# The output norm of a tuned encoder block: gains loaded once and multiplied on GpSimd, the last scaling split over VectorE and ScalarE

## Chip, cores, metric

One core of one Trainium2 chip runs the whole kernel. The metric is device time in microseconds, the median of several runs. Engines are called TensorE (PE in the profile), VectorE (DVE), ScalarE (ACT), GpSimd (POOL) and SyncE (SP, which only issues transfers here).

## What is computed

One encoder layer on x of 1 x 2048 x 1024 in float32: an RMS norm, one wide projection, two branches (chunked attention over a band, and retention with a per-head norm), each gated and multiplied by its own output matrix, a gated merge, an output projection with the residual, and a last RMS norm. The change touches the last two lines of this:

```python
def rms_norm(x, gain):
    xf = x.astype(jnp.float32)
    y = xf * lax.rsqrt(jnp.mean(xf * xf, axis=-1, keepdims=True) + NORM_EPS)
    return (y * gain.astype(jnp.float32)).astype(x.dtype)

        branch_a = jnp.einsum('bsf,fd->bsd', o_a * jax.nn.silu(g_a), w_out_attn[l])
        branch_r = jnp.einsum('bsf,fd->bsd', o_r * jax.nn.silu(g_r), w_out_ret[l])
        mixed = jax.nn.sigmoid(m_a) * branch_a + jax.nn.sigmoid(m_r) * branch_r
        x = x + jnp.einsum('bsd,de->bse', mixed, w_out[l]).astype(x.dtype)
    return rms_norm(x, final_gain)
```

## The kernel before

Every matmul keeps float32 accuracy by splitting its operands in a high and a low part (a cast on ScalarE, then a subtraction on VectorE), and the large products are tiled 512 wide. The phases run one behind the other: projections, attention and retention for the first half of the sequence's work, the same for the second, then the merge, opened by `open_phase("mrg", E_MRG, 4)`. The merge runs five jobs in this order: ba0 (attention branch, first half), br0 (retention branch, first half), ba1, br1, and the output projection `out`. Each job goes through chunks of weights. A chunk loads a raw weight tile (`raw`, in a ring of 3), casts it to `wh` (L295, ScalarE) and subtracts to get `wl` (L296, VectorE); its products are 128 x 512, 24 matmuls each in `out`. The names in the traces: raw_ba and wh_ba, wl_ba belong to ba0 and ba1, raw_br and wh_br, wl_br to br0 and br1; ps_ba, ps_br, ps_out are the products in PSUM.

The right operands r lie on chip and are refilled while the phase runs: `refill` (L777 to 782) loads a piece from `yrs` into the low part, casts it (L781) and subtracts (L782). The retention's result passes through `finish_yr` (loads yr, yv, rb, a multiply on VectorE, one on GpSimd at L1067, a store to yrs). The epilogue of a branch product (L1088 for ba) multiplies PSUM with a gate tile ga, which is stored to `tas`; the one of br (L1106, L1107) multiplies with gr and adds ta on GpSimd, and is stored to `mxs`.

The epilogue of an output product is `ep_out` (L1138 to 1158). `before_out` has loaded the rows of x (xr) and the gain (fg, one 1 x 512 piece broadcast to 128 rows), both from ring E. VectorE adds the product to xr (L1143), ScalarE squares and sums into a column of fs (L1149). When the second half of a row block is there, VectorE makes mean and epsilon (L1153, L1154), runs `rsqrt` (L193 to 203, nine small operations: L195, L199, L196, then L202 and L203 three times) and multiplies each half by the result and by the gain (L1158). `put` stores it six steps later, or at the end of the program.

What sets the order: the program is written out step by step while it is recorded. `later(n, fn)` puts a piece of work n steps behind the present one, `put(lag, ...)` a store, and `flush` at the end of a phase emits what is left. Nearly all transfers of this part are issued by SP, in the order in which they were recorded (`dma`); an issue that has to wait holds all behind it. Ring E has E_MRG buffers of 128 x 512 float32 in the merge, and the tiles ga, gr, ta, yr, yv, rb, xr, fg, jk go through it. Before the merge the phase `heads(1)` ends with a chain of operations on rt on VectorE (per-head norm of the retention) and the store of its result to `rss`, which `finish_yr` later loads as rb.

Of the kernel before, what the change touches and what calls it, by code (L numbers as in the profile page):

```python
# [11 lines left out]
F32 = mybir.dt.float32  # L12
# [4 lines left out]
ALU = mybir.AluOpType  # L17
AX = mybir.AxisListType
# [3 lines left out]
P = 128  # L22
SEQ = 2048
DM = 1024
# [9 lines left out]
NORM_EPS = 1e-6  # L34
# [17 lines left out]
E_PROJ = 23  # L52
E_ATT = 16
E_RET = 22
E_MRG = 23
PR_BUFS = 4
ATT_FILLS = (1.0, 1.0)
PV_LAG = 3
# [11 lines left out]
def hybrid_kernel(  # L70
# [24 lines left out]
    small = ctx.enter_context(tc.tile_pool(name="small", bufs=4))  # L95
# [3 lines left out]
    epool, xpool = [None], [None]  # L99
# [10 lines left out]
    def E(name, dt=F32, shape=(P, 512)):  # L110
        return epool[0].tile(list(shape), dt, tag="e", name=name)
# [7 lines left out]
    def open_phase(name, e_bufs, tr_bufs=0):  # L119
        st = ExitStack()  # L120
        phase[0] = st
        epool[0] = st.enter_context(tc.tile_pool(name=f"e_{name}", bufs=e_bufs, reuse_waits="tile"))
        if tr_bufs:
            xpool[0] = st.enter_context(
                tc.tile_pool(name=f"tr_{name}", bufs=tr_bufs, space=PSUM, reuse_waits="tile")
            )
        return st
# [21 lines left out]
    pe, act, dve, pool = Ordered(nc.tensor), Sometimes(nc.scalar), Sometimes(nc.vector), Sometimes(nc.gpsimd)  # L149
    dma = Ordered(nc.sync).dma_start  # L150
# [42 lines left out]
    def rsqrt(v, y, tmp, hv):  # L193

        dve.tensor_scalar(tmp.bitcast(I32), v.bitcast(I32), 1, None, ALU.logical_shift_right)  # L195
        dve.tensor_scalar(  # L196
            y.bitcast(I32), tmp.bitcast(I32), -1.0, RSQRT_MAGIC, ALU.mult, ALU.add
        )
        dve.tensor_scalar(hv, v, -0.5, None, ALU.mult)  # L199
        if v.shape[-1] == 1:  # L200
            for _ in range(3):
                dve.scalar_tensor_tensor(tmp, y, hv, y, ALU.mult, ALU.mult)  # L202
                dve.scalar_tensor_tensor(y, tmp, 1.5, y, ALU.add, ALU.mult)  # L203
            return
        for _ in range(3):
            dve.tensor_tensor(tmp, y, hv, ALU.mult)
            dve.tensor_tensor(tmp, tmp, y, ALU.mult)
            dve.scalar_tensor_tensor(y, tmp, 1.5, y, ALU.add, ALU.mult)
# [32 lines left out]
    def later(n, fn):  # L241

        order[0] += 1
        deferred.append((steps[0] + n, order[0], fn, free[0]))
        deferred.sort(key=lambda e: e[:2])
# [8 lines left out]
    def put(lag, dst, src):  # L254

        later(lag, lambda: dma(dst, src))
# [799 lines left out]
    def finish_yr(h, b, lead):  # L1056

        a, u, r = (E(f"{n}_{h}_{b}") for n in ("yr", "yv", "rb"))
        dma(a, orscr[h // 2][b][h % 2])
        dma(u, urscr[h][b])  # L1060
        dma(r, rsscr[b // 2][8 * b + h].rearrange("(o d) -> o d", o=1).broadcast_to([P, B]))

        def gated():
            dve.scalar_tensor_tensor(a, a, gn[:, h:h + 1], u, ALU.mult, ALU.mult)

        def rest():
            pool.tensor_tensor(a, a, r, ALU.mult)  # L1067
            put(6, yrscr[h][b], a)

        later(lead, gated)  # L1070
        later(lead + 2, rest)
# [52 lines left out]
        b, u = c // 2, c % 2  # L1124
        return mxscr[b][4 * j:4 * j + 4, :, T * u:T * u + T].rearrange("k p t -> p k t")

    rows_out = {}

    def before_out(c, i, j):
        t = 2 * c + j  # L1130
        xr, fg = E(f"xr_{t}_{i}"), E(f"fg_{t}_{i}")
        dma(xr, x[0, t * P:(t + 1) * P, 512 * i:512 * i + 512])
        dma(
            fg, final_gain[512 * i:512 * i + 512].rearrange("(o d) -> o d", o=1).broadcast_to([P, 512]),
        )
        return xr, fg

    def ep_out(c, i, j, src, got):  # L1138

        t = 2 * c + j  # L1140
        xr, fg = got

        dve.scalar_tensor_tensor(xr, src, 0.25, xr, ALU.mult, ALU.add)  # L1143
        if t not in rows_out:
            rows_out[t] = ({}, small.tile([P, 2], F32, tag="fs", bufs=4, name=f"fs_{t}"))
        halves_, fs = rows_out[t]
        halves_[i] = xr, fg
        junk = E(f"jk_{t}_{i}", BF16)
        act.activation(junk, xr, AF.Square, accum_out=fs[:, i:i + 1])  # L1149
        if len(halves_) < 2:  # L1150
            return
        ft, fr, tm, hv = (small.tile([P, 1], F32, tag=f"f{n}", bufs=2, name=f"f{n}_{t}") for n in range(4))
        dve.tensor_reduce(ft, fs, AX.X, ALU.add)  # L1153
        dve.tensor_scalar(ft, ft, 1.0 / DM, NORM_EPS, ALU.mult, ALU.add)  # L1154
        rsqrt(ft, fr, tm, hv)
        for f in range(2):
            o, fg = halves_[f]
            dve.scalar_tensor_tensor(o, o, fr, fg, ALU.mult, ALU.mult)  # L1158
            put(6, out[0, t * P:(t + 1) * P, 512 * f:512 * f + 512], o)


    def attention(s, sbp, ps_wide):
# [442 lines left out]
    for s in range(2):  # L1605
        jobs.append(Job(f"ba{s}", 4, w_stream(w_out_attn, [T * c for c in range(4)], 1), ep_ba(s),
                        kh=1, resident=RYA, before=before_ba(s)))
        jobs.append(Job(f"br{s}", 4, w_stream(w_out_ret, [T * c for c in range(4)]), ep_br(s),
                        resident=RYR, before=before_br(s)))
    jobs.append(Job("out", 8, mx_stream, ep_out, resident=RWO, before=before_out))  # L1610
    end, at = {}, 0
    for j in jobs:
# [82 lines left out]
    strict[0] = False  # L1695

    st = open_phase("mrg", E_MRG, 4)
    for n, (b, h) in enumerate((b, h) for b in range(2, 4) for h in range(HEADS)):
        later(YR_FROM + YR_EVERY * n, lambda h=h, b=b: finish_yr(h, b, 8))
    while step():  # L1700
# [63 lines left out]
```

## Time and profile before

| | |
|---|---|
| time of the runs | 1994.56, 1995.48, 1995.9 us; median 1995.48 us |
| the profiled execution | 1991.62 us, its span from first to last instruction 1989.8 us |
| mean granted clock of TensorE | 0.994 |
| busy share of the span | TensorE 97%, VectorE 69%, ScalarE 45%, GpSimd 44% |
| merge | about 1560 to 1990 us, its out stage 1807.6 to 1981.7 us |

The profile gives, for one execution, what each engine did and when, what ended an idle time (a "releaser"), and a chain followed back from the last instruction. Times in rows are microseconds from the start of the span. A row with x2 or x3 groups neighbouring instructions of the same kind.

### The profile page before, as it was taken

To read this page: it belongs to the slowest core of one execution; us is meant where nothing else is said; L and a number is where in the kernel's file an instruction comes from. 1 tells how busy PE (TensorE), PEld (TensorE's weight loads), DVE (VectorE), ACT (ScalarE), POOL (GpSimd) and SP (SyncE) were. 2 spreads that over 40 slices of the span, in tenths; PEclk is the share of its full clock that TensorE was granted. 3 is DMA by queue.
4 is the path that set the end of the run, shared out by engine and by line. 5 is a ranking of instruction groups with operands and counts; after the bars stand their busy time and mean duration, and the time that the engine had idled before them with its cause. 6 is when DMAs were issued, how large, how long until landed. Compare 5 with 4: busy or idle time off the path is not lost.

```text
span 1989.8 us, 30314 instructions
## 1 busy us (share of the span) xinstructions
PE 1926.7 (97%) x9712; PEld 1604.4 (81%) x9712; DVE 1365.6 (69%) x2603; ACT 899.6 (45%) x1827; POOL 878.7 (44%) x713
## 2 busy tenths in 40 slices
PE   6899999999999999999999999999999999999998
PEld 4687778888888886778788888888888887888886
DVE  7888777777765668888877677765667654534554
ACT  6444554556654555343333555554455311322221
POOL 2544554554556675455654444454675144021000
PEclk9899999999999999999999999999999999999999
DMA  4476796755549987777775645544899999976564
GB/s 148 136 255 210 225 301 205 207 156 165 173 115 282 296 262 259 232 254 237 250 254 173 192 144 168 169 146 137 268 289 281 332 383 372 342 241 216 194 191 138
DMA packets 340910, 447.44 MB, mean 225 GB/s; under 512 B 30776, under 2 KB 194256, under 8 KB 340752
## 3 DMA queue, kind: packets, MB, share of 16 engines
q1 hardware_dynamic: 282688, 388.87, 61.2%
q10 hardware_dynamic: 58064, 56.63, 9.5%
q8 instruction: 78, 1.28, 0.3%
q14 instruction: 80, 0.66, 0.1%
HBM read 294.50 MB, written 150.89 MB: 224 GB/s over the span
## 4 chain that ended last, share of the span: by engine, by line
PE 75%; DVE 9%; DMA 8%; issue 3%; ACT 2%; POOL 2%; SPq 0%; DVEq 0%; ACTq 0%; POOLq 0%
PE ps_g_z L139 7%; PE ps_g_x L139 6%; PE ps_p_z L139 5%; PE ps_p_x L139 5%; PE po L139 4%; PE ps_g_w L139 4%; PE wide L139 4%; PE ps_g_v L139 3%; PE ps_g_y L139 3%; PE o L139 3%; PE tp L139 2%; PE ps_p_w L139 2%; PE ps_p_y L139 2%; PE ps_p_v L139 2%; PE sr L139 1%
## 5 line engine op out<-in xcount | busy, mean ns | idle before, releaser
L139 POOL TENSOR_SCALAR pr<-pr,rsum 128x640 f32<-128x640 f32 (+4 forms) x128 | 97.5, 762 | 233.9 <-DVE rsum L139 99.9
L139 PE MATMUL ps_p_z<-r,wh_p 128*128 128x512 f32 x448 | 145.1, 404 | 6.8 <-DVE u_p L139 5.5
L139 DVE CUSTOM_DVE_ANT_0 pr<-wide,bt 128x640 f32<-128x640 f32 (+4 forms) x128 | 94.3, 736 | 73.7 <-PE wide L139 63.3
L139 PE MATMUL ps_g_z<-r,wh_g 128*128 128x512 f32 x448 | 142.4, 399 | 1.9 <-DVE c_g L139 1.5
L139 PE MATMUL ps_g_x<-r,wh_g 128*128 128x512 f32 x448 | 142.6, 399 | 0.0
L139 PE MATMUL ps_p_x<-r,wh_p 128*128 128x512 f32 x448 | 141.4, 396 | 1.1 <-DVE r L139 1.0
L139 ACT ACTIVATE pr<-pr,mn 128x640 f32<-128x640 f32 (+4 forms) x128 | 98.0, 766 | 80.1 <-DVE mn L139 80.1
L139 POOL TENSOR_TENSOR t_p<-raw_p,t_p 128x512 f32<-128x512 f32 x52 | 78.0, 1501 | 123.7 <-DVE wl_p L139 111.7
L139 DVE TENSOR_TENSOR ptl<-tp,pth 128x384 fp32r<-128x384 f32 x168 | 95.8, 571 | 37.1 <-ACT pth L139 35.5
L139 ACT CAST pth<-tp 128x384 fp32r<-128x384 f32 x168 | 85.5, 515 | 76.2 <-PE tp L139 69.0
L139 POOL TENSOR_TENSOR sl<-sm,sh 128x512 fp32r<-128x512 f32 x64 | 89.2, 1394 | 44.5 <-ACT sh L139 30.9
L1107 POOL TENSOR_TENSOR gr<-gr,ta 128x512 f32<-128x512 f32 x32 | 45.5, 1422 | 140.2 <-DVE gr L1106 135.1
L139 PEld LDWEIGHTS ps_p_z<-r,wh_p 128*128 128x128 f32 x448 | 83.7, 193 | 24.9 <-issue 6.3
L139 DVE TENSOR_TENSOR wl_p<-t_p,wh_p 128x512 fp32r<-128x512 f32 x112 | 101.9, 910 | 1.6 <-ACT wh_p L139 1.6
L139 PEld LDWEIGHTS ps_p_x<-r,wh_p 128*128 128x128 f32 x448 | 83.5, 189 | 19.7 <-DVE r L139 2.6
L139 PEld LDWEIGHTS tp<-ident,pr 128*128 128x128 f32 x560 | 69.6, 140 | 36.8 <-DVE ptl L139 9.0
L139 PE MATMUL tp<-ident,pr 128*128 128x128 f32 x560 | 90.0, 274 | 7.8 <-DVE g L139 2.9
L139 PE MATMUL wide<-ka,qa 128*128 128x512 f32 (+2 forms) x448 | 94.0, 326 | 0.7 <-DVE mn L139 0.7
L139 PE MATMUL po<-pth,va 128*128 128x256 f32 x336 | 92.7, 297 | 0.0
L139 PE MATMUL ps_p_z<-r,wl_p 128*128 128x512 f32 x224 | 89.2, 398 | 0.3 <-DVE wl_p L139 0.3
L139 POOL TENSOR_TENSOR wl_g<-t_g,wh_g 128x512 fp32r<-128x512 f32 x56 | 75.7, 1351 | 31.2 <-ACT wh_g L139 31.1
L139 PE MATMUL ps_p_x<-r,wl_p 128*128 128x512 f32 x224 | 87.9, 393 | 1.0 <-DVE wl_p L139 1.0
(1183 smaller groups left out, 5835.7 us busy)
## 6 DMA issues: line engine op xcount, KB each, us to landing
raw_g<-in_w_in_dram ACTq DMA_DIRECT2D x56, 512.0 KB, 5.4
raw_p<-in_w_in_dram ACTq DMA_DIRECT2D x52, 512.0 KB, 6.2
qa<-qas SPq DMA_DIRECT2D x128, 128.0 KB, 2.9
qr<-qrs SPq DMA_DIRECT2D x128, 128.0 KB, 4.4
vr<-vrs SPq DMA_DIRECT2D x64, 256.0 KB, 5.5
ka<-kas SPq DMA_DIRECT2D x40, 256.0 KB, 3.5
va<-vas SPq DMA_DIRECT2D x40, 256.0 KB, 3.2
kds<-kdt_k SPq DMA_DIRECT2D x32, 256.0 KB, 4.2
```

The source lines that it names most:

```text
L139: return tc.keep_in_program_order(op(*a, **k))
L1107: pool.tensor_tensor(g, g, ta, ALU.add)
```

## The change

The gain is loaded once, at the start of the merge, as two tiles of 128 x 512 with a buffer each, and multiplied by the square root of the width on ScalarE. The 32 loads of fg in `before_out` are gone, and E_MRG is 21 instead of 23, which pays for the two tiles. In `ep_out` GpSimd multiplies each half of xr by its gain into a tile og of ring E, beside the squares. One operation with two columns replaces the sum and the mean (the mean's divisor is in the scaled gain). Half 0 is multiplied by the rsqrt on VectorE, half 1 on ScalarE. The very last store is issued by ScalarE, all others by SP as before.

```diff
-E_MRG = 23
+E_MRG = 21
...
+    def load_gains():
+        for i in range(2):
+            fg = epool[0].tile([P, 512], F32, tag=f"fg{i}", bufs=1, name=f"fg_{i}")
+            gains.append(fg)
+            dma(
+                fg, final_gain[512 * i:512 * i + 512].rearrange("(o d) -> o d", o=1).broadcast_to([P, 512]),
+            )
+            later(14, lambda fg=fg: act.mul(fg, fg, DM ** 0.5))
...
     def before_out(c, i, j):
-        xr, fg = E(f"xr_{t}_{i}"), E(f"fg_{t}_{i}")
+        xr = E(f"xr_{t}_{i}")
         dma(xr, x[0, t * P:(t + 1) * P, 512 * i:512 * i + 512])
-        dma(
-            fg, final_gain[512 * i:512 * i + 512].rearrange("(o d) -> o d", o=1).broadcast_to([P, 512]),
-        )
...
         act.activation(junk, xr, AF.Square, accum_out=fs[:, i:i + 1])
+        og = E(f"og_{t}_{i}")
+        pool.tensor_tensor(og, xr, gains[i], ALU.mult)
+        halves_.append(og)
...
-        dve.tensor_reduce(ft, fs, AX.X, ALU.add)
-        dve.tensor_scalar(ft, ft, 1.0 / DM, NORM_EPS, ALU.mult, ALU.add)
+        dve.scalar_tensor_tensor(ft, fs[:, 0:1], DM * NORM_EPS, fs[:, 1:2], ALU.add, ALU.add)
         rsqrt(ft, fr, tm, hv)
+        dve.tensor_scalar(halves_[0], halves_[0], fr, None, ALU.mult)
+        act.mul(halves_[1], halves_[1], fr)
         for f in range(2):
-            o, fg = halves_[f]
-            dve.scalar_tensor_tensor(o, o, fr, fg, ALU.mult, ALU.mult)
-            put(6, out[0, t * P:(t + 1) * P, 512 * f:512 * f + 512], o)
+            dst = out[0, t * P:(t + 1) * P, 512 * f:512 * f + 512]
+            if t == SEQ // P - 1 and f:
+                act.dma_start(dst, halves_[f])
+            else:
+                put(6, dst, halves_[f])
...
     st = open_phase("mrg", E_MRG, 4)
+    load_gains()
```

The order on the engines moves with it. SP at the start of the merge, before; here r31 and r21 are refilled from yrs, rss is the retention's row chain, and raw_ba0_3 the last weight tile of ba0:

```order
L139 DMA r31_88<-yrs_0_1_327 128x512
L139 DMA ga_4_0_18058<-mas_4_0_374 128x512
L139 DMA r31_88<-yrs_1_1_331 128x512
L139 DMA raw_ba0_3_0_18093<-in_w_out_attn_dram 128x4x256
L139 DMA ga_4_1_18095<-mas_4_1_375 128x512
L139 DMA r31_88<-yrs_3_1_339 128x512
L139 DMA ga_5_0_18115<-mas_5_0_378 128x512
L139 DMA rss_1_464<-rt0_17990 32x512
L139 DMA tas_3_0_434<-ga_3_0_18006 128x512
L139 DMA tas_3_1_435<-ga_3_1_18029 128x512
L139 DMA tas_4_0_438<-ga_4_0_18058 128x512
```

and the same place on SP now:

```order
L139 DMA r31_88<-yrs_0_1_327 128x512
L139 DMA ga_4_0_18058<-mas_4_0_374 128x512
L139 DMA r31_88<-yrs_1_1_331 128x512
L139 DMA rss_1_464<-rt0_17990 32x512
L139 DMA tas_3_0_434<-ga_3_0_18006 128x512
L139 DMA tas_3_1_435<-ga_3_1_18029 128x512
L139 DMA fg_0_18091<-in_final_gain_dram 128x512
L139 DMA fg_1_18093<-in_final_gain_dram 128x512
L139 DMA r31_88<-yrs_2_1_335 128x512
L139 DMA raw_ba0_3_0_18097<-in_w_out_attn_dram 128x4x256
L139 DMA ga_4_1_18099<-mas_4_1_375 128x512
L139 DMA r31_88<-yrs_3_1_339 128x512
```

The store of rss, two of tas and the two gain loads now stand ahead of raw_ba0_3, ga_4_1, yrs_3_1 and (not in these rows) ga_5_0; the load from yrs_2_1, which stood some 35 places earlier before, is behind them too.

VectorE at the same place, now; wl_ba0_3 is made from raw_ba0_3, and the lines L1088 are epilogues of ba0:

```order
L139 TENSOR_TENSOR wl_ba0_2_(1, 0)_18056<-raw_ba0_2_0_17969,wh_ba0_2_(1, 0)_18055 128x512
L1088 SCALAR_TENSOR_TENSOR ga_4_0_18058<-ga_4_0_18058,ps_ba0_2_(0, 0)_18101 128x512
L782 TENSOR_TENSOR r31_88<-r31_88,r30_87 128x512 x2
L296 TENSOR_TENSOR wl_ba0_3_(0, 0)_18117<-raw_ba0_3_0_18097,wh_ba0_3_(0, 0)_18116 128x512
L1088 SCALAR_TENSOR_TENSOR ga_4_1_18099<-ga_4_1_18099,ps_ba0_2_(0, 1)_18121 128x512
L296 TENSOR_TENSOR wl_ba0_3_(1, 0)_18164<-raw_ba0_3_0_18097,wh_ba0_3_(1, 0)_18163 128x512
```

Two subtractions of L782 have come in front of wl_ba0_3; the epilogue of ga_4_1 stands right behind that subtraction, as it did.

VectorE at the very end, now, from the last two epilogues on:

```order
L1150 SCALAR_TENSOR_TENSOR xr_15_0_21396<-ps_out_7_(1, 0)_21447,xr_15_0_21396 128x512
L1150 SCALAR_TENSOR_TENSOR xr_15_1_21445<-ps_out_7_(1, 1)_21480,xr_15_1_21445 128x512
L1162 SCALAR_TENSOR_TENSOR f0_15_21510<-fs_15_21475 128x1
L195 TENSOR_SCALAR f2_15_21512<-f0_15_21510 128x1
L199 TENSOR_SCALAR f3_15_21513<-f0_15_21510 128x1
L196 TENSOR_SCALAR f1_15_21511<-f2_15_21512 128x1
L202 SCALAR_TENSOR_TENSOR f2_15_21512<-f1_15_21511,f3_15_21513 128x1
```

The row L1162 has taken the place of L1153 and L1154. At the end of ScalarE's order stand now the scaling of half 1 and the last store:

```order
L1155 ACTIVATE jk_15_0_21476,fs_15_21475<-xr_15_0_21396 128x512
L1155 ACTIVATE jk_15_1_21506,fs_15_21475<-xr_15_1_21445 128x512
L1165 ACTIVATE og_15_1_21508<-og_15_1_21508,f1_15_21511 128x512
L1169 DMA out_0_dram<-og_15_1_21508 128x512
L1773 UNCONDITIONAL_BRANCH
```

Before, the squares (jk_15_1) were the last work of ScalarE.

## Rows read from the trace of the kernel before

**Rows 1.** The page: busy time by engine.
```profile
PE 1926.7 (97%) x9712; PEld 1604.4 (81%) x9712; DVE 1365.6 (69%) x2603; ACT 899.6 (45%) x1827; POOL 878.7 (44%) x713
```
**Rows 2.** Waits of TensorE, 1560 to 1990: for what, total us, times, longest.
```profile
PE ps_br_(0, 0)_18876 L139 <- ACT wh_br_(0, 0)_18799 L295: 1.5, 1, 1.5
```
**Rows 3.** Busy us by stretch: PE, PEld, DVE, ACT, POOL, clock, DMA share, GB/s.
```profile
1570.00:1585.00 15.00, 15.00 (x67) 12.41 (x67) 9.28 (x16) 4.14 (x7) 1.30 (x1) 1.00 0.87 293
1590.00:1655.00 65.00, 63.54 (x279) 51.97 (x278) 31.42 (x41) 10.16 (x17) 27.86 (x21) 1.00 1.05 384
1807.60:1981.70 174.10, 174.07 (x768) 143.79 (x767) 89.66 (x258) 40.06 (x91) 1.67 (x1) 1.00 0.57 183
```
**Rows 4.** The chain that ended last, from 1981 on: start, us, what.
```profile
1981.71 0.70 DVE xr L1143
...
1983.19 0.17 DVE f L1153
...
1985.29 0.75 DVE xr L1158
1986.04 0.66 DVEq L1760
```
**Rows 5.** The last stores on SP: start, us, what.
```profile
1986.06 0.99 SPq L139 DMA_DIRECT2D out_dram<-xr  x2
```
**Rows 6.** Groups by shape: count, busy us, mean ns, idle before.
```profile
L139 DVE TENSOR_SCALAR xb<-xb,n_b 128x512 f32<-128x512 f32 x4 | 1.7, 482 | 0.0
L139 ACT ACTIVATE xb<-xb,n_b 128x512 f32<-128x512 f32 x4 | 2.6, 712 | 2.3 <-DVE n_b L139 2.3
L202 DVE SCALAR_TENSOR_TENSOR f<-f,f 128x1 f32<-128x1 f32 x48 | 10.5, 220 | 1.7
```
**Rows 7.** GpSimd and VectorE around 1616: start, us, what.
```profile
1616.17 1.29 POOL L1107 TENSOR_TENSOR gr<-gr,ta 128x512 f32<-128x512 f32 x1 [2.43 <-DVE gr L1106]
1616.67 1.33 DVE L1064 SCALAR_TENSOR_TENSOR yr<-yr,gn,yv 128x512 f32<-128x512 f32 x1 [0.58 <-DMA yv<-urs]
```
**Rows 8.** TensorE at 1576, 1587 and 1654: start, us, what.
```profile
1576.63 0.62 PE L139 MATMUL ps_ba_(0, 0)_18195<-r,wh_ba_(0, 0)_18112 128*128 128x512 f32 x2
1587.51 0.62 PE L139 MATMUL ps_br_(0, 0)_18300<-r,wh_br_(0, 0)_18211 128*128 128x512 f32 x2
1654.68 0.73 PE L139 MATMUL ps_br_(0, 0)_18876<-r,wh_br_(0, 0)_18799 128*128 128x512 f32 x2 [1.46 <-ACT wh_br_(0, 0)_18799 L295]
```
**Rows 9.** SP's issues at the start of the merge: start, us, what.
```profile
1563.12 0.44 SPq L139 DMA_DIRECT2D raw_ba<-in_w_out_attn_dram  x1
...
1569.72 0.32 SPq L139 DMA_DIRECT2D rss<-rt  x1
1570.08 1.75 SPq L139 DMA_DIRECT2D tas<-ga  x3
...
1572.42 0.41 SPq L139 DMA_DIRECT2D r<-yrs  x1
1573.58 0.32 SPq L139 DMA_DIRECT2D tas<-ga  x1
1573.99 0.38 SPq L139 DMA_DIRECT2D r<-yrs  x1
...
1578.50 1.53 SPq L139 DMA_DIRECT2D raw_br<-in_w_out_ret_dram  x2
```
**Rows 10.** VectorE: the first subtraction of raw_ba0_3 and the epilogue of ga_4_1.
```profile
1572.26 0.69 DVE L296 TENSOR_TENSOR wl_ba_(0, 0)_18113<-raw_ba,wh_ba_(0, 0)_18112 128x512 fp32r<-128x512 f32 x1 [0.77 <-ACT wh_ba_(0, 0)_18112 L295]
1572.87 0.68 DVE L1088 SCALAR_TENSOR_TENSOR ga<-ga,ps_ba_(0, 1)_18117 128x512 f32<-128x512 f32 x1
```
**Rows 11.** ScalarE's casts that waited for a load: start, us, what.
```profile
1575.43 0.62 ACT L781 CAST r<-r 128x512 fp32r<-128x512 f32 x1 [2.69 <-DMA r<-yrs]
1578.46 0.62 ACT L781 CAST r<-r 128x512 fp32r<-128x512 f32 x1 [2.41 <-DMA r<-yrs]
...
1585.85 0.62 ACT L295 CAST wh_br_(0, 0)_18211<-raw_br 128x512 fp32r<-128x512 f32 x1 [0.96 <-DMA raw_br<-in_w_out_ret_dram]
```

More of the change, by code (lines that the diff above doesn't have):

```diff
@@ L1125, in mx_stream @@
         return mxscr[b][4 * j:4 * j + 4, :, T * u:T * u + T].rearrange("k p t -> p k t")
-    rows_out = {}
+    rows_out, gains = {}, []
+    def load_gains():
[6 more added lines that the diff above has]
+            later(14, lambda fg=fg: act.mul(fg, fg, DM ** 0.5))
     def before_out(c, i, j):
         t = 2 * c + j
-        xr, fg = E(f"xr_{t}_{i}"), E(f"fg_{t}_{i}")
+        xr = E(f"xr_{t}_{i}")
         dma(xr, x[0, t * P:(t + 1) * P, 512 * i:512 * i + 512])
-        dma(
-            fg, final_gain[512 * i:512 * i + 512].rearrange("(o d) -> o d", o=1).broadcast_to([P, 512]),
-        )
-        return xr, fg
+        return xr
     def ep_out(c, i, j, src, got):
         t = 2 * c + j
-        xr, fg = got
+        xr = got
         dve.scalar_tensor_tensor(xr, src, 0.25, xr, ALU.mult, ALU.add)
         if t not in rows_out:
-            rows_out[t] = ({}, small.tile([P, 2], F32, tag="fs", bufs=4, name=f"fs_{t}"))
+            rows_out[t] = ([], small.tile([P, 2], F32, tag="fs", bufs=4, name=f"fs_{t}"))
         halves_, fs = rows_out[t]
-        halves_[i] = xr, fg
         junk = E(f"jk_{t}_{i}", BF16)
         act.activation(junk, xr, AF.Square, accum_out=fs[:, i:i + 1])
+        og = E(f"og_{t}_{i}")
+        pool.tensor_tensor(og, xr, gains[i], ALU.mult)
+        halves_.append(og)
         if len(halves_) < 2:
```

## The prediction, made before the changed kernel ran

> **What bounds the kernel now.** I read the page first. TensorE is busy 97% of the span, the next engine 69% [rows 1]; the granted clock is 1.00, the 2.4 GHz level, in every stretch of [rows 3]. So only two things can move the time: a gap in TensorE's stream, or the work behind its last matmul. I then asked for everything that TensorE waited for from 1560 us to the end, which covers the rest of the retention and the whole merge: one wait, 1.5 us, for a cast of a weight tile [rows 2]. The out stage, where the changed norm sits, runs without a gap: 174.07 us busy in 174.10 [rows 3]. VectorE, ScalarE and GpSimd are busy 52%, 23% and 1% there. What the change takes from VectorE in that stage, and the 32 gain loads that it drops, therefore buys nothing, except behind the last matmul.
>
> Two places are left. **The tail**: the last matmul ends at 1981.7 and the span at 1989.8, so 8.1 us lie bare [rows 4]. **The start of the merge**: from 1590 to 1655 the DMA engines are full (share 1.05, 384 GB/s), and the one wait of TensorE, at 1654.68, is for a weight load that came out of that full queue [rows 2, 3, 8]. A transfer that starts later before 1590 comes out later at 1654. From 1570 to 1585 the share is 0.87, so there is some idle there [rows 3].
>
> **The tail, step by step** [rows 4 to 6]. Before: the epilogue from 1981.71 for 0.70, the squares on ScalarE, the first small operation at 1983.19, ten more of them, scaling of half 0 from 1985.29 for 0.75, its store, scaling of half 1, and the last store (1986.06 and, 0.66 behind the end of half 0, about 1986.7; the two issues fill 0.99). From the last issue to the end are 3.1 us.
> - Of the two operations that make the mean (each 0.17, and gaps of 0.02; they end at 1983.54) one goes; the other becomes a two-input one, which takes 0.17 to 0.22 [rows 4, 6]. Alone that gains 0.14 to 0.19.
> - But GpSimd now multiplies the last half beside the squares. It starts some 0.06 behind the epilogue, at 1982.47, takes 1.29 as in [rows 7], and ends at 1983.76, while the first small operation would start at 1983.19. A row of the merge shows what happens to a VectorE operation of the scalings' kind (0.75 alone [rows 4]) that starts inside such a multiply [rows 7]: begun at 1616.67, it took 1.33 and ended 0.54 after the multiply's end at 1617.46. It did most of its work once GpSimd was through. The small operation reads two columns of SBUF, so I let it wait too. With its whole length behind the multiply it ends at 1983.95, with the 0.2 that the row saved (0.75 - 0.54) at 1983.76; I take 1983.9, where the pair of before ended at 1983.54. The chain is 0.35 *late* instead of 0.17 early; the nine operations behind it run as before, and the rsqrt ends at about 1985.6. The Trainium skill ("SBUF — State Buffer", on the two sides of SBUF) has the rule behind this: a VectorE instruction with two SBUF inputs and a GpSimd instruction that reads SBUF share a port pair, which the one that starts first keeps for its whole length. The row agrees at 512 columns; none shows it for one column, and if that is exempt the tail is 0.5 better than I put it.
> - Half 0: 0.48 on VectorE, by the tensor-by-column rows on 128x512 [rows 6], in place of 0.75, and its store at about 1986.1.
> - Half 1 beside it on ScalarE: 0.71 by the same scaling of 128x512 in the first phase [rows 6]. Done at about 1986.35, and the store is issued by ScalarE's queue, free then, at 1986.37 in place of 1986.7.
> - The other 31 multiplies lie in a stage in which GpSimd is idle. ScalarE's 16 added multiplies (16 x 0.7 = 11 us) lie in 134 us of idle time, and each holds the casts queued behind it for the two to three microseconds of a rsqrt chain, with 5.44 us of TensorE work (174.1/32) for each product in front.
> - What a store from ScalarE's queue costs at the end isn't in the trace: at best as from SP's, at worst some 0.5 more (two issues of SP fill 0.99). I take nothing more, since the bytes are the same.
>
> The tail gains 0.35; ends: 0.2 lost, and 1.2 gained with no hold and a quicker landing of two stores side by side.
>
> **The start of the merge, step by step.** Keeping the gains on chip costs two loads at the phase's start, and these and E_MRG at 21 move other loads. Before, SP issues the load of the last weight tile of the first branch (raw_ba0_3) at 1563.12, with three more loads (ga_4_1, yrs_3_1, ga_5_0), then stands still until 1569.72, when the retention's last row chain has ended on VectorE and rss can be stored [rows 9]. By the order of the built program that store and two of tas, then the two gain loads, now stand *ahead* of these loads, and the load of yrs_2_1 as well, which had been issued long before. Nothing else fills SP's idle time, so five loads (4 x 256 KB and 512 KB) go out later, four of them by some 9.5 us.
> - SP's issues after the stop follow each other at about 0.5 us [rows 9]: rss 1569.72, tas 1570.1 and 1570.6, gains 1571.1 and 1571.6, yrs_2_1 1572.1, raw_ba0_3 1572.6 in place of 1563.1.
> - When does it land? The loads of yrs issued at 1572.42 and 1573.99 had their casts released at 1575.43 and 1578.46 [rows 9, 11], 3.0 and 4.5 us after; raw_ba0_3 is twice as large, so 4.0 to 5.5, I take 4.6: 1577.2. From landing to the first matmul takes 0.7 (a cast of 0.62 [rows 11] and two hand-overs), so 1577.9 against 1576.63 before: TensorE stands 1.3 us there (0.5 to 2.2).
> - On VectorE the subtraction for that tile now stands ahead of ga_4_1's epilogue as before, but waits for it; with the cast at 1577.2, the subtraction follows after 0.65 and the epilogue ends some 1.45 after that starts (1572.26 and 1572.87 with 0.68 before [rows 10]), so at about 1579.3 in place of 1573.55. SP's store of ga_4_1 (tas_4_1) waits for it, and behind that on SP wait the next yrs, ga_6_0, the three loads of the next row, and then the first weight tile of the second branch (raw_br0_0). Before, that store went at 1573.58 and raw_br0_0 at 1578.50 [rows 9], 4.9 later; so it goes at about 1584.2, 5.7 later.
> - What it does to the stream: after 1569.7 the engines have to move 1.5 MB of the five loads and 0.5 MB of gains more ahead of raw_br0_0: 2.1 MB at 384 GB/s, 5.4 us. The idle share from 1570 to 1585, (1.05 - 0.87) x 15 / 1.05 = 2.6 us [rows 3], can take some of it, if SP feeds it. All of it used: the stream is 2.8 late; none used: 5.4. SP is blocked for about 3 us, with some six loads in flight to live on, so I lean to the lower end: 3.2.
> - Before, raw_br0_0 was cast at 1585.85 and wanted at 1587.51 [rows 8, 11], with its weights ready some 0.7 after the cast starts, at 1586.5; 3.2 later that is 1589.7, and TensorE, by then 1.3 late itself, wants it at 1588.8: 0.9 of a wait, 2.2 in all. From there to 1655 the full queue decides: the tile awaited at 1654.68 comes 3.2 later, whatever TensorE lost on the way; the stall there becomes 1.5 + 3.2 - 2.2 = 2.5, or part of it falls on the tiles between. Behind it TensorE waited for nothing [rows 2], so 3.2 reaches the end.
>
> **The sum.** 3.2 - 0.35 = 2.85 us more. The profiled execution takes 1991.62 (span 1989.8), so 1994.5; the median of the runs shown, 1995.48, lies 3.9 above it, and so 1998.3 for the time. A change of under 0.2% (4 us: 1991.5 to 1999.5) can't be told from none here.
>
> **Rivals.**
> A, slower: SP's stop drains the queue. If loads behind the stop take what raw_br0_0 took (issued 1578.50, cast 1585.85: 7.3 us), raw_ba0_3 lands at 1579.9, ga_4_1's epilogue ends at 1582, raw_br0_0 goes at 1586.9 and its cast comes at 1592 (queue filling) to 1594 (queue full), 6 to 8 late; two buffers fewer in the ring push the same way. With 6.4 the sum is +6.05: 2001.5. It decides from a stream 4.3 late on. For it: each step on this path waits for the one ahead, and the queue is full right after. Against it: the 7.3 us are those of a full queue, and behind the stop the rows show 3.0 to 4.5.
> B, absorbed: raw_ba0_3 lands by 1575.9, as the 3.0 us row would give with the idle engines, nobody waits for it, the epilogue of ga_4_1 and so SP's store come at most a few microseconds late, and the stream recovers before 1654. Only the tail counts: 1995.1. For it: 2.6 us of idle share. Against it: 2.1 MB don't fit into that.
> C, the tail is not held: the small operation runs beside the multiply, the rsqrt ends at 1985.1, ScalarE's half at 1985.85, and the tail gains 0.85: 1997.8. For it: the row is not of one column. Against it: the row of two inputs.
>
> **How the numbers follow.** Forecast (the stream 2.5 to 4.3 late, the tail held): 0.42. A 0.30, B 0.17, C 0.11. Time 1998.3. Range: B's 1995.1 less C's 0.5 gives 1994.6; above, A up to a stream 6.8 late, 2001.9. Faster by over 0.2% needs 4 us, and all that could be gained is the tail's 1.2 and the stall's 1.5: 0.04. Slower by over 0.2%: A and the forecast's upper edge, 0.32. Within: 0.64.
>
> **What would show it.** At the start: SP's gap before rss stays, the gain loads stand behind it, raw_ba0_3 is issued near 1572.6, a wait of TensorE of 0.5 to 2 us near 1577 for its cast, another near 1588, and the wait near 1656 for the second branch's last tile moves from 1.5 to about 2.5. The out stage still 174.1 us without a gap. In the tail: a first small operation of 0.7 in place of 0.15 that ends 0.2 behind the multiply, ten small operations in place of eleven, two scalings that overlap, a last issue on ScalarE 4.7 us behind the last matmul in place of 5.0. Wrong: no new wait before 1600 (B), waits of TensorE there that add up to over 4.3 us more than before (A), a first small operation of 0.2 (C), or a gap in the out stage, for which I see no reason.

## Result and the profile after

The changed kernel takes 2002.88 us, the one before in the same runs 1995.69: 1.0036 times as long, with a 95% interval of 1.0023 to 1.005, some 7 us. I had said 1998.3 with a range up to 2001.9, and "no difference that can be told" as the likeliest class. The time lies 1 us above the range, and beyond the 2001.5 of rival A. The profiled execution has a span of 1999.6, 9.8 longer than that of before.

Where it is: nearly all of it between the retention's end and the last weight tile of br0, which TensorE takes up at 1654.68 before and at 1663.60 now. TensorE's waits from 1560 on in the changed kernel (for what, total us, times, longest), five in place of the one of [rows 2]:

```profile
PE ps_ba_(0, 0)_18201 L139 <- ACT wh_ba_(0, 0)_18116 L295: 2.8, 1, 2.8
PE ps_br_(0, 0)_18882 L139 <- ACT wh_br_(0, 0)_18805 L295: 1.5, 1, 1.5
PE ps_br_(0, 0)_18306 L139 <- ACT wh_br_(0, 0)_18217 L295: 0.9, 1, 0.9
PE ps_br_(0, 0)_18698 L139 <- ACT wh_br_(0, 0)_18614 L295: 0.6, 1, 0.6
PE ps_ba_(0, 0)_19124 L139 <- ACT wh_ba_(0, 0)_19054 L295: 0.3, 1, 0.3
```

SP at the start of the merge, the answer to [rows 9] (start, us, what; the last row is from SP's waits there: for what, total us, times, longest):

```profile
1571.36 0.33 SPq L139 DMA_DIRECT2D rss<-rt  x1
1571.73 0.92 SPq L139 DMA_DIRECT2D tas<-ga  x2
1572.77 0.88 SPq L139 DMA_DIRECT2D fg<-in_final_gain_dram  x2
...
1574.20 0.42 SPq L139 DMA_DIRECT2D raw_ba<-in_w_out_attn_dram  x1
...
1578.29 0.32 SPq L139 DMA_DIRECT2D r<-yrs  x1
1582.50 0.32 SPq L139 DMA_DIRECT2D tas<-ga  x1
...
1586.75 1.27 SPq L139 DMA_DIRECT2D raw_br<-in_w_out_ret_dram  x2
...
SPq L139 <- DVE ga L1088: 3.5, 1, 3.5
```

ScalarE's casts of the two weight tiles, the answer to [rows 11]:

```profile
1580.54 0.62 ACT L295 CAST wh_ba_(0, 0)_18116<-raw_ba 128x512 fp32r<-128x512 f32 x1 [0.91 <-DMA raw_ba<-in_w_out_attn_dram]
...
1594.35 0.62 ACT L295 CAST wh_br_(0, 0)_18217<-raw_br 128x512 fp32r<-128x512 f32 x1 [0.96 <-DMA raw_br<-in_w_out_ret_dram]
```

Stretches of 2.5 us there in the kernel before (the last three columns: granted clock, DMA share, GB/s):

```profile
1567.50:1570.00 2.50, 2.50 (x12) 2.07 (x12) 2.50 (x5) 0.30 (x1) 0.00 (x0) 1.00 0.82 301
1570.00:1572.50 2.50, 2.50 (x12) 2.07 (x12) 1.73 (x4) 1.42 (x3) 0.00 (x0) 1.00 0.76 263
```

and in the changed kernel, with the out stage, to be read against [rows 3]:

```profile
1567.50:1570.00 2.50, 2.50 (x12) 2.07 (x12) 2.50 (x5) 0.62 (x1) 0.00 (x0) 1.00 0.02 6
1570.00:1572.50 2.50, 2.50 (x12) 2.07 (x12) 2.50 (x6) 0.00 (x0) 0.00 (x0) 1.00 0.10 25
...
1580.00:1582.50 2.50, 1.29 (x3) 0.80 (x4) 1.67 (x4) 1.76 (x3) 0.00 (x0) 0.82 1.05 397
1582.50:1585.00 2.50, 2.50 (x7) 1.98 (x6) 2.38 (x4) 0.62 (x1) 0.00 (x0) 0.50 0.91 297
1585.00:1587.50 2.50, 2.50 (x12) 2.03 (x11) 1.88 (x3) 0.62 (x1) 0.00 (x0) 1.00 0.89 305
1587.50:1590.00 2.50, 2.50 (x13) 2.07 (x12) 0.73 (x2) 0.00 (x0) 0.00 (x0) 1.00 0.82 196
1817.00:1991.40 174.40, 174.40 (x770) 144.16 (x768) 84.61 (x227) 50.74 (x106) 44.75 (x32) 1.00 0.41 137
```

The places in the program move against each other from execution to execution: rss is issued anywhere between 1569.7 and 1576.9 in the profiles of this study, whatever the kernel, so 1.6 of the 9.8 (1571.36 against 1569.72) belong to no change. I therefore measure from the issue of rss. The first cast of raw_br0_0 comes 22.99 after it, in place of 16.13 (1594.35 - 1571.36, 1585.85 - 1569.72). The first matmul with the last tile of br0, at 1663.60, comes 92.24 after it in place of 84.96: 7.3 later, the loss that the runs show. From there to the last matmul the changed kernel takes 327.85 in place of 327.02, of which a new wait is 0.3; runs below without such a wait take 327.0 (e4) to 328.6 (e2), so the rest is no sign of the change. The out stage has no gap: 174.40 busy in 174.40. And the tail, from the start of VectorE's last epilogue to the end of the span, takes 8.13 in place of 8.09.

The tail's rows, the answer to [rows 4 and 5]:

```profile
1991.47 0.69 DVE L1150 SCALAR_TENSOR_TENSOR xr<-ps_out_(1, 1)_21480,xr 128x512 f32<-128x512 f32 x1 [4.75 <-PE ps_out_(1, 1)_21480 L139]
...
1992.40 1.26 POOL L1157 TENSOR_TENSOR og<-xr,fg 128x512 f32<-128x512 f32 x1 [4.15 <-DVE xr L1150]
...
1992.95 0.72 DVE L1162 SCALAR_TENSOR_TENSOR f<-fs 128x1 f32<-128x1 f32 x1 [0.79 <-ACT jk L1155]
...
1995.49 0.72 ACT L1165 ACTIVATE og<-og,f 128x512 f32<-128x512 f32 x1 [2.57 <-DVE f L203]
1995.51 0.49 DVE L1164 TENSOR_SCALAR og<-og,f 128x512 f32<-128x512 f32 x1
1996.02 0.33 SPq L139 DMA_DIRECT2D out_dram<-og  x1
1996.24 0.37 ACTq L1169 DMA_DIRECT2D out_dram<-og  x1
```

### The profile page after: what moved, and what is told of

Same layout as the page of the kernel before. It is cut to its first block, busy times and chain, and to the rows that moved or that the text cites. A ratio compares the mean times of both kernels' runs of the same rounds, so it can differ in the third digit from the quotient of the medians.

```text
span 1999.6 us, 30345 instructions
## 1 busy us (share of the span) xinstructions
PE 1928.4 (96%) x9712; PEld 1602.4 (80%) x9712; DVE 1357.3 (68%) x2571; ACT 912.4 (46%) x1845; POOL 919.7 (46%) x745
## 4 chain that ended last, share of the span: by engine, by line
PE 74%; DMA 9%; DVE 9%; issue 3%; ACT 2%; POOL 1%; SPq 1%; ACTq 0%; DVEq 0%; POOLq 0%
PE ps_g_z L139 7%; PE ps_g_x L139 6%; PE ps_p_z L139 5%; PE ps_p_x L139 5%; PE po L139 4%; PE ps_g_w L139 4%; PE wide L139 3%; PE ps_g_v L139 3%; PE ps_g_y L139 3%; PE o L139 3%; PE ps_p_w L139 3%; PE tp L139 2%; PE ps_p_y L139 2%; PE ps_p_v L139 2%; PE sr L139 1%
## 5 line engine op out<-in xcount | busy, mean ns | idle before, releaser
L1157 POOL TENSOR_TENSOR og<-xr,fg 128x512 f32<-128x512 f32 x32 | 44.3, 1386 | 129.4 <-DVE xr L1150 94.5
L139 DVE TENSOR_TENSOR sm<-sr,dm 128x512 f32<-128x512 f32 x64 | 44.1, 689 | 67.4 <-PE sr L139 31.9
```

The costliest lines, as they stand in the source:

```text
L139: return tc.keep_in_program_order(op(*a, **k))
L1157: pool.tensor_tensor(og, xr, gains[i], ALU.mult)
```

## Experiments

Theory S: the whole loss is the start of the merge, where the first weight tiles now stand on SP behind the retention's row chain. Rivals: fewer buffers (F), the output stage or the tail (O), the bytes of two more loads at that place, or that they are broadcasts. In the table, "behind rss" is the time from the issue of rss to the first cast of raw_br0_0, and to the first matmul with the last tile of br0. The ratio is taken over the runs and is not the quotient of the two medians; e5 was run once.

| kernel | time, before beside it | ratio, 95% interval | cast behind rss | matmul behind rss |
|---|---|---|---|---|
| before | 1995.69 | | 16.13 | 84.96 |
| changed | 2002.88 | 1.0036, 1.0023 to 1.005 | 22.99 | 92.24 |
| e1_gains_late | 1996.67, 1996.49 | 1.0003, 0.9989 to 1.0016 | 15.55 | 83.81 |
| e2_gains_only | 2003.39, 1996.49 | 1.0042, 1.0027 to 1.0056 | 23.52 | 91.87 |
| e3_gains_8 | 1998.23, 1996.49 | 1.0013, 1.0001 to 1.0025 | 16.85 | 86.52 |
| e4_emrg21 | 1994.71, 1996.49 | 1.0001, 0.999 to 1.0012 | 16.67 | 85.60 |
| e5_late_sp | 1995.15, 1995.33 | | 15.75 | 83.74 |
| e6_tail_free | 1994.37, 1995.33 | 1.0007, 0.999 to 1.0024 | 16.43 | 84.61 |
| e8_before_rss_act | 1995.01, 1995.33 | 0.9997, 0.9984 to 1.0009 | 15.84 | 84.60 |
| e9_gains_act | 1996.92, 1995.33 | 1.0007, 0.9996 to 1.0019 | 16.62 | 85.01 |
| e10_dve_half | 1994.15, 1995.88 | 0.9996, 0.9978 to 1.0013 | 16.52 | 84.99 |
| e11_plain | 2001.49, 1995.88 | 1.0032, 1.002 to 1.0045 | 22.84 | 92.47 |
| e12_lag | 2006.99, 1995.48 | 1.0063, 1.0051 to 1.0075 | 21.65 | 97.03 |
| e13_before_lag | 2004.12, 1995.48 | 1.0045, 1.0032 to 1.0058 | 16.59 | 92.01 |

**The whole change, with the gain loads recorded later** (e1).

```diff
-    load_gains()
+    later(260, load_gains)
```

> The whole change, but the two gain loads are recorded 260 steps later, shortly ahead of the output projection; the order at the start of the merge is then that of before. Theory S (the whole loss is the start of the merge: the first weight tiles stand behind the retention's row chain): time within 2 us of before, 1994 to 1997, no wait of TensorE near 1577, last branch tile awaited near 1655. Rival F (fewer ring buffers) and rival O (output stage or tail with its GpSimd and ScalarE work): still 5 to 8 us slower, about 2002. Tail: from the last matmul to the end 8.1 to 8.2 us as in the changed kernel, since the first small operation is still held by the multiply.

The loss is gone, with 21 buffers, GpSimd's multiplies and the split scaling all in place; TensorE waits once, 0.6 us, at the last tile of br0. Rivals F and O fall.

**Only the gain loads, in the kernel before** (e2). `E_MRG = 21`, `load_gains()` at the start of the merge, and the epilogue of before, with its own 32 loads.

> Before, with only the two gain tiles loaded and scaled at the start of the merge and 21 buffers; they are not used, and the output norm is that of before. Theory S: 6 to 8 us slower than before (2002 to 2004), with a wait of about 2.8 us near 1578 and a lower granted clock behind it. Rival O: as before, 1995.5. Rival F: slower, but without a wait near 1578.

The whole loss is there. The wait is 2.7, and the matmuls behind it run at a granted 0.50, the 1.2 GHz level, for one stretch, as in the changed kernel. The 32 loads, the norm and the tail have no part in it.

**Fewer buffers alone** (e4): `E_MRG = 21` in the kernel before.

> Before with 21 buffers in the ring in place of 23 and nothing else; the order on every engine is that of before. Theory S: within 1 us of before. Rival F: 3 us or more slower, with waits of SP for buffers in the merge.

No difference, and SP issues in the order of before. The front section's sentence that ga, gr and ta go through ring E was wrong: they lie in another ring, so E_MRG bounds less of the merge than I had it.

**Order or bytes.** First (e3) `later(8, load_gains)`: the gain loads stand behind raw_ba0_3 and rss, ahead of raw_br0_0.

> The whole change, with the gain loads recorded 8 steps later: behind raw_ba0_3 and rss, but still ahead of raw_br0_0. It tells the order apart from the bytes. Theory S as order: the first wait near 1578 is gone, and only the two loads' own transfer time, 2 x 0.65 us, delays the stream ahead of raw_br0_0: 0.5 to 2 us slower than before. If the two loads themselves cost the 7 us (a broadcast that transfers slowly), this kernel is still 5 us or more slower.

1.6 later by the rows, 1.7 by the medians (the interval of the ratio allows 0.2 to 5.0), where two transfers of 0.67 (256 KB at 390 GB/s) make 1.3. Then (e9) the loads at the place of the change, but on ScalarE's queue (`act.dma_start` in `load_gains`):

> The whole change, with the two gain loads at the start of the merge as in it, but issued by ScalarE's queue. SP's order at the start of the merge is then that of before: raw_ba0_3 ahead of rss. The bytes and the stage are those of the change. Theory S as order: within 2 us of before, with no wait near 1577. If the bytes at this place are the cost: 5 us or more slower.

Within what can be told, with no wait near 1577. Its SP issues show the order that the change had turned round, raw_ba0_3 ahead of rss:

```profile
1565.51 0.44 SPq L139 DMA_DIRECT2D raw_ba<-in_w_out_attn_dram  x1
1572.14 0.32 SPq L139 DMA_DIRECT2D rss<-rt  x1
```

So of the 7.3 the two loads by themselves cost between nothing (e9) and 1.6 (e3), and their place in SP's order the rest, some 5.7 or more. SP issues in the order that the built program fixes. Recorded first in the phase, the gain loads were put behind the retention's last store, and what is recorded behind them on SP came behind that store with them; on ScalarE's queue they pull nobody along. Why the built program sets them behind that store stays open.

**Broadcast or not** (e11). e2 with two loads of 128 rows of x in place of the broadcasts:

```diff
-            dma(
-                fg, final_gain[512 * i:512 * i + 512].rearrange("(o d) -> o d", o=1).broadcast_to([P, 512]),
-            )
+            dma(fg, x[0, 0:P, 512 * i:512 * i + 512])
```

> Before with 21 buffers and two loads at the start of the merge in SP's order, but of 128 rows of x instead of the one row of gains sent to 128 partitions; the tiles are scaled and not used, the output norm is that of before. It tells whether raw_ba0_3 landed 6.2 to 6.3 us after its issue (in place of my 4.6) because the two loads ahead of it are broadcasts. If so: 4.5 to 5 us here, a wait of TensorE near 1578 of about 1.2, and a loss of 4 to 5. If a broadcast costs what any load of 256 KB costs: 6.2, a wait of 2.7 and 6 to 8 us slower than before, as with the gains.

Half of each. From issue to cast raw_ba0_3 takes 5.1 (1577.63 to 1582.74) in place of e2's 6.2, and the two loads ahead of it land 3.3 and 3.4 after their issue in place of 4.6 and 4.9. So in these two profiles the broadcasts hold up what stands behind them by about 1.1, and the first wait falls to 1.6, with the clock at 1.00 behind it. But the cast of raw_br0_0 comes 22.84 behind rss, close to e2's 23.52, and most of the loss stays (1.0032 against 1.0042, with intervals that overlap). TensorE's waits are now:

```profile
PE ps_br_(0, 0)_18306 L139 <- ACT wh_br_(0, 0)_18217 L295: 3.4, 1, 3.4
PE ps_ba_(0, 0)_18201 L139 <- ACT wh_ba_(0, 0)_18116 L295: 1.6, 1, 1.6
```

What the first wait no longer takes, the second one does. It is the stream of transfers that sets the loss, not the first wait.

**SP's second stop** (e12, and e13 as its control). In the changed kernel SP stands from 1578.6 on for 3.5 at the store of ga_4_1, whose epilogue is behind the late tile. With `put(12, ...)` in place of `put(4, ...)` for the stores of tas, that store goes behind raw_br0_0:

> The whole change, gain loads at the start of the merge as in it, but the stores of tas recorded 12 steps behind their epilogue in place of 4. In SP's order the store of ga_4_1 then stands behind raw_br0_0 and cannot hold it; raw_ba0_3 still stands behind rss and the gains (and now behind two more stores). Theory (SP's second stop, at the store that waits for the late epilogue, delays the stream): the first wait of TensorE stays at 2.5 to 4 us, raw_br0_0 is issued some 10 to 11 us behind rss in place of 15.4, and the loss falls from 7 to 2 to 4 us. Rival (the first wait and the clock behind it are the loss): still 5 to 7.

> Before, with the same 12 steps for the stores of tas: the control for the run above. raw_ba0_3 stays ahead of rss. Expected within 1.5 us of before; if it gains or loses, the run above is to be read against it.

This came out otherwise. The control loses 8.6 by itself: up to 1660 its SP waits 15.9, in 13 places, for stores of tas to land, where the kernel before waits 0.8. So the comparison is between these two. They differ by 2.9 in the medians and 5.0 in the matmul behind rss (97.03 - 92.01); e12's first wait is 5.1, above the 2.5 to 4 expected. The stop is gone in e12, yet raw_br0_0 is issued 15.5 behind rss, as with the stop (15.4): from 1575 to 1588 SP waits 4.7 for transfers in flight instead, at most 1.2 at a time. The DMA engines are full there, where the changed kernel had 0.91, 0.89 and 0.82:

```profile
1582.50:1585.00 2.50, 0.86 (x3) 0.46 (x3) 1.57 (x3) 1.41 (x4) 0.00 (x0) 0.87 1.05 388
1585.00:1587.50 2.50, 2.50 (x7) 2.02 (x7) 2.50 (x5) 1.03 (x3) 0.00 (x0) 0.50 1.05 387
1587.50:1590.00 2.50, 2.50 (x12) 1.98 (x12) 2.50 (x5) 0.61 (x1) 0.00 (x0) 0.95 1.04 389
```

So with the transfers moved behind rss, and no stop at that store, the cast is 5.1 late (21.65 - 16.59), and the stop would be worth the remaining 1.8 of 6.9. That last figure compares two pairs of kernels and is an argument, not a measurement.

**The stop at rss itself** (e8): the store of rss on ScalarE's queue, in the kernel before.

> Before, with the store of rss issued by ScalarE's queue in place of SP's. SP no longer stands still for the retention's row chain; the two stores of tas still wait for epilogues. If the stop itself is what costs TensorE its 1.5 us near 1655: up to 1.5 us faster, 1994 to 1995.5. If the stores behind it stop SP just as long: no difference.

No difference, and the wait at the last tile of br0 is 1.4. But SP is not freed: from 1560 to 1580 it waits 5.7, in three places, for epilogues of VectorE whose results it has to store. So this run shows only that moving the store of rss alone gains nothing; what a free SP would be worth there was not tried.

**The tail.** Three kernels on top of e1. First the last store on SP (e5), then the second half of the last block without GpSimd (e6: VectorE applies rsqrt and gain in one operation), then only the last multiply by the gain on VectorE (e10), whose edit is:

```diff
-        pool.tensor_tensor(og, xr, gains[i], ALU.mult)
+        (dve if t == SEQ // P - 1 and i else pool).tensor_tensor(og, xr, gains[i], ALU.mult)
```

> The kernel with the late gain loads, and the last store issued by SP like all the others. From the last matmul to the end it was 8.1 us with the store on ScalarE, as before the change, though that store was issued 0.25 earlier. If a store from ScalarE's queue takes longer to the end than one from SP's, SP's store, issued at about the same time, ends the span 0.2 to 0.3 earlier: 7.85. If two stores at a time share the engines and the end is set by their sum, it stays at 8.1.

> The late gain loads, and in the last row block only the second half is not multiplied on GpSimd: VectorE multiplies it by the rsqrt and the gain in one operation, while ScalarE scales the first half and issues its store. Nothing of GpSimd lies beside the last small operations. Theory (the multiply holds the first of them, by 0.55): that operation takes about 0.2 in place of 0.73, and from the last matmul to the end it is 7.3 to 7.6 us in place of 8.1. Rival (the operation is slow by itself, since it has two inputs): 0.7 again, 8.1. The time: 1995 to 1996.5, a difference that only the profile can tell.

> The whole change with the late gain loads, and only the very last multiply by the gain (half 1 of the last row block) on VectorE in place of GpSimd. VectorE is idle for 0.78 while ScalarE squares, and the multiply takes 0.69. Theory: the first small operation takes 0.16 and starts at once, the rsqrt ends 0.55 earlier than in the changed kernel, the first store follows 3.9 after VectorE's last epilogue starts, the last 4.15. If the end follows the first store by 3.55 and the last by at least 3.1, the span ends 7.45 after that epilogue starts, in place of 8.1: 0.6 us better than before. Rival: the store's issue on ScalarE ends later (3.36 after issue): 7.5. Time 1994.5 to 1996, not told from before by the runs.

All from the start of VectorE's last epilogue: changed kernel 8.13, e1 and e5 8.09, e6 7.80, e10 7.60. I had expected 7.3 to 7.6 of e6 and 7.45 of e10. The five profiles with the epilogue and tail of before (e2, e4, e8, e11, e13) have 7.93 to 8.12, so a difference of 0.2 is no more than chance here. The hold is real: without GpSimd beside it the same operation takes 0.16, in e6 and e10. From e10:

```profile
1988.90 0.69 DVE L1150 SCALAR_TENSOR_TENSOR xr<-ps_out_(1, 1)_21480,xr 128x512 f32<-128x512 f32 x1 [4.75 <-PE ps_out_(1, 1)_21480 L139]
1989.63 0.69 DVE L1157 TENSOR_TENSOR og<-xr,fg 128x512 f32<-128x512 f32 x1
...
1990.38 0.16 DVE L1162 SCALAR_TENSOR_TENSOR f<-fs 128x1 f32<-128x1 f32 x1
...
1992.88 0.33 SPq L139 DMA_DIRECT2D out_dram<-og  x1
1993.11 0.37 ACTq L1169 DMA_DIRECT2D out_dram<-og  x1
```

In e10 the last store goes 4.21 behind that epilogue's start, 0.80 sooner than in the kernel before, and the span ends 0.49 sooner: the rest is lost at the stores. From the first store's issue to the end it is 3.57 to 3.76 in the six kernels with the output stores of before, whose second follows 0.66 later, and 3.54 to 3.62 in the eight others, whose second follows within 0.5, on either queue (e5 1989.76 to 1993.3, e6 1986.68 to 1990.3, e10 1992.88 to 1996.5, changed 1996.02 to 1999.6). A second store that comes closer wins 0.2 at most. That the two share the engines fits this (share 1.03 at 389 GB/s from 1997 to 1998 in the changed kernel) but was not tried by itself. e5, where SP issues both, ends no later than e1.

e10 is the best version here: 0.5 us less tail than before by the profile. In the runs it is 0.9996, 0.9978 to 1.0013, so no difference that can be told. e1, e6 and e10 undo the loss; none of them beats the kernel before by a measurable amount.

## Why the prediction was wrong

**What bounds the kernel**: right. The out stage has no gap with 32 more multiplies on GpSimd and 16 on ScalarE, and of the two places that I named, the start of the merge is where the time moved; the tail kept its length (8.13 against 8.09).

**The start of the merge, order and issues**: right. rss, two tas, the gains, yrs_2_1 and raw_ba0_3 are issued in that order, raw_ba0_3 2.84 behind rss (I had 2.9). e1, e2 and e9 show that this order is the loss. What I blamed on E_MRG beside it is nothing (e4).

**Landing of raw_ba0_3**: too short. I had 4.6 from the yrs rows; it took 6.3 from issue to cast, and the wait is 2.8 in place of 1.3. Of the 1.7, about 1.1 are the broadcasts ahead of it (e11: 5.1). A nearer row was there: in the trace of before the eight loads of raw_ba land 5.5 to 6.7 after their issue, 5.7 in the median.

**What I left out**: behind the wait of 2.8 the granted clock fell to 0.50 for a stretch, and the first product took 4.56 (1581.20 to 1585.76) where the next took 2.72. That is 1.8 more, not in my working. It didn't set the end, since TensorE still waited 1.5 for the stream at the last tile.

**The stream**: this is the step that failed. I put its lateness between 2.8, all idle share of the DMA engines used, and 5.4, none used, and leaned to 3.2, because "some six loads in flight" would bridge SP's stop. Measured: 6.9 at raw_br0_0's cast, 7.3 at the last tile. Of the 3.7 that I was short at the cast, 0.9 are the issue of raw_br0_0 (15.4 behind rss, where I had 14.5) and 2.8 its way from issue to cast: it took 7.6, as 7.3 before, and I had let it land in 4.9, though the nine transfers ahead of it go out at 0.47 apiece and the engines move one in about 0.67 (256 KB at 390 GB/s).

Not only was none of the idle used, the change made more of it: the engines stand nearly still from 1567.5 to 1572.5 (0.02 and 0.10, where the kernel before has 0.82 and 0.76), since the loads that used to be in flight there are gone, and run at 0.82 to 0.91 from 1582.5 to 1590. e12 against e13, without SP's second stop, gives 5.1, near my upper end. Rival A had the size (6.4), and its reason, a queue drained by the stop at rss, is what these stretches show. Its price for the load behind the stop was too high (7.3; raw_ba0_3 took 6.3), and so was its sign: TensorE's waits before 1600 add up to 3.7 (2.8 + 0.9), not to over 4.3. The second stop, at the store of ga_4_1, is the smaller part as far as e12 and e13 can tell.

**The way through to the end**: right. The full queue carries the delay to 1655, whatever TensorE lost on the way, and the wait there stays at 1.5 while earlier ones take the rest.

**The tail**: the hold was right (first small operation 0.72, its end 2.20 behind the epilogue's start; I had 2.2), and so against rival C. The last store went 4.77 behind that start in place of 5.01, but the gain of 0.35 did not arrive: 8.13 against 8.09. The mis-sized term is the end of two stores at a time, which I took as 3.1 behind the last one and which took 3.36; the last store itself went 0.24 sooner, not 0.35.

**Chances**: 0.32 for slower by over 0.2% was too low for a chain of three steps, each of which waits for the one ahead. The range's upper end used a stream of 6.8; 7.3 and no gain in the tail make 2002.8.

## To carry to other kernels

A load put into a queue whose order is fixed costs not only its own transfer: it can pull everything recorded behind it to the place where it is put itself. Look for what was in flight during the queue's next stop, and count the bytes that are put off as late one for one, unless the trace shows the engines fed during the gap. A load with nothing urgent in it belongs late, or on a queue on which nobody waits.

## What the runs showed of the hardware that I had not expected

A one-column VectorE operation with two SBUF inputs waits for a GpSimd multiply as a 512-column one does: at the end it takes 0.72 in place of 0.16, in each of the profiles that has the multiply beside it (changed, e1, e3, e5, e9, e12). The changed kernel's out stage shows the same without any second kernel. The operation occurs 16 times there, once for each row block: five times it begins after the multiply has ended and takes 0.14 to 0.15, and eleven times it begins inside the multiply, takes 0.59 to 1.22 and ends within 0.02 of the multiply's end. One of each (start, us, what):

```profile
1829.11 1.61 POOL L1157 TENSOR_TENSOR og<-xr,fg 128x512 f32<-128x512 f32 x1 [4.15 <-DVE xr L1150]
1829.76 0.98 DVE L1162 SCALAR_TENSOR_TENSOR f<-fs 128x1 f32<-128x1 f32 x1 [0.19 <-ACT jk L1155]
...
1850.86 1.30 POOL L1157 TENSOR_TENSOR og<-xr,fg 128x512 f32<-128x512 f32 x1 [4.14 <-issue]
1852.64 0.15 DVE L1162 SCALAR_TENSOR_TENSOR f<-fs 128x1 f32<-128x1 f32 x1
```

The rule that the Trainium skill ("SBUF — State Buffer", on the two sides of SBUF) states for such pairs, that whichever starts first has the shared ports for its whole length, agrees at this size too.

A gain row sent to 128 partitions delays what stands behind it more than a plain load of the same 256 KB: 1.1 us over two loads (6.2 in e2 against 5.1 in e11 from issue to cast of raw_ba0_3), and the two land 4.6 and 4.9 after their issue in place of 3.3 and 3.4. Each is one execution; in the changed kernel it was 6.3, and 4.6 and 5.0.

TensorE's granted clock fell to 0.50, the 1.2 GHz level, or within 0.01 of it, for one or two stretches of 2.5 us behind waits of 2.7 (e2), 2.8 (changed), 3.0 (e13), 3.4 (e11) and 5.1 (e12), and stayed at 1.00 behind one of 1.6 (e11).
